# A gMLP and dilated-attention trunk: q stored with bare sums of squares, its statistics made in the attention; layer A's low halves one step later; operand tiles in another order

## The chip, the cores and the metric

The kernel runs on one core of a Trainium2 chip. The metric is the device time of one execution in microseconds (us), as the median over runs. PE is TensorE's matmul side and PEld its weight load, DVE is VectorE, ACT is ScalarE, POOL is GpSimd, and SP is the engine whose queue issues nearly all DMAs of this kernel.

## The reference

One batch of 2048 tokens with 1024 features passes through a gMLP layer A and a layer B of attention in three dilated groups. All is float32. Cut to what matters here:

```python
def gmlp_layer(x, ...):                     # layer A, width 2048
    shift, scale, gate = ada_mod(c, ada_w, ada_b, 3)
    h = rms_norm(x, norm_g) * (1 + scale) + shift
    u, v, z = jnp.split(h @ w_in, 3, axis=-1)
    v = rms_norm(jax.nn.gelu(v), sgu_g)     # then mixed within chunks of 128 tokens
    y = jax.nn.gelu(u) * mixed * jax.nn.silu(z)
    return x + gate * (y @ w_out)

def dilated_layer(x, c, kv_groups, ...):    # layer B; groups (128, 1), (512, 4), (2048, 16)
    shift, scale, gate = ada_mod(c, ada_w, ada_b, 3)
    h = rms_norm(x, norm_g) * (1 + scale) + shift
    qz = h @ w_in                           # 24 heads of 128 for q, then z of 1024
    q = rms_norm(q, q_norm_g) * (HEAD_DIM ** -0.5)
    for g, (window, d) in enumerate(DILATED_GROUPS):
        o, lse = dilated_group_attn(q[:, :, hs], kb, vb, slopes[hs], window, d)
    alpha = softmax(lse over the groups)
    y = sum(alpha * o) * jax.nn.silu(z)
    return x + gate * (y @ w_out)
```

Between them stands one projection to keys and values that all groups of layer B share. The scores of a head are q.k plus minus slope times distance, under a mask of 128 keys. `rms_norm` of q divides each head's row by the root of the mean of its squares plus 1e-6: this is the statistic that the change moves.

## The kernel before

**Blocks and stages.** The 2048 tokens are taken in four blocks of 512, Q = 0 to 3. For each block `layer_A` makes v, u, z, the mixing and the output product; then `proj_B` makes, in this order, `kv_block(2)`, `kv_block(1)`, `q_block(2)`, `kv_block(0)`, `q_block(1)`, `q_block(0)` and `z_block`. A number behind `q_block` is the group of the attention. The q and z projections and layer A's output product are `dense_s`: a product of 2 x 2 blocks with seven products in place of eight, in the order "11", "s2", "12", "s3", "s1", "22", "s4"; its seven operands lie in four large tiles of the pool `big` (`new_ops`), two in a tile. Each product is three matmuls (`mm3`), since operand and weight are each split into a high half and a low half. Layer A's operand is made ahead by `make_hA`, in pieces: `norm_T` transposes and scales two of the eight feature tiles, ACT writes the high half hAh (L615) and DVE subtracts for the low half hAl (L617).

**Weights.** `raw_unit` loads 128 x 512 of a weight into a tile named raw (L264; six buffers), and `split` has ACT copy it to the high half (L255) and DVE subtract for the low half (L259) into a tile named w (eight buffers); the names tell which weight: w_z0b is the z projection of Q = 0, w_q31t of Q = 3 the q projection of group 1. A "t" at such a name's end marks a sum of weight blocks, read from the array wt; in pd_z0bb, the products' sums in PSUM, the last letter tells one of two pairs.

**Storing q.** When `dense_s` has a 128 x 512 piece of q (four heads) it calls `ev` in `q_block`. ACT squares the piece (L1039), DVE sums the squares of each head (L1041), and POOL makes four small operations (L1042 to L1045): times 1/128 plus 1e-6, to the power -0.5, the product of both, and that times the slope. The last results lie in columns 512 to 519 beside the piece, in one tile st of 520 columns. The tile's store to the array qd in HBM goes to a list, `pending`; `flush` (L251) issues what is in the list behind the weight loads of the next product, so on SP the stores of q stand among the loads of weights. SP issues in order: a DMA whose semaphores aren't there yet holds up all behind it. z goes the same way, without statistics.

**The attention.** One unit is a block of 128 queries, four heads. `att_q` loads its qt of 520 columns from qd (L1129), `att_1` transposes it on PE (pq, L1150) and copies the statistics to a small tile rt on DVE (L1160). `att_2` makes the scores (L1182), adds the distance times rt (L1191), takes the maximum (L1194, L1195) and the exponential on ACT (L1201), scaled by rt. `att_3` transposes the result (pp, L1242), and `att_4` multiplies by the values (po, L1261). Groups 0 and 1 of block Q - 1 (`attend_local`) run beside layer A of block Q; group 2, 32 units, runs beside `kv_block(0)`, `q_block(1)` and `q_block(0)` of Q = 3, and block 3's own groups 0 and 1 at the end, in `finish`, with the output projection, whose weights `load_wo` brings from the array wob.

**Who sets the order.** Such work beside the main one is a generator in the list `fillers`; `tick`, called between the matmuls of a dense product, runs so many steps of it as `rate` says. `weave(main, side)` gives a step of the side work to each step of the main one. So the order on every engine follows from where a generator is put in the list, and a scheduler orders what may go beside each other by priority and by the buffers that are free. The gate of layer B, gb, is such side work: `ada_gate` loads eight tiles aw_gb of 128 x 2 x 512 (L170) and sums them on DVE (L172, L174); in this kernel it goes with `proj_B` of Q = 1. `gate_out`, which needs it, is woven into `attend_local(1)`, beside layer A of Q = 2.

Of the kernel before, what the change touches and what calls it, by code (L numbers as in the profile page):

```python
# [12 lines left out]
F32 = mybir.dt.float32  # L13
F32R = mybir.dt.float32r
AF = mybir.ActivationFunctionType
ALU = mybir.AluOpType
AX = mybir.AxisListType

P = 128
# [7 lines left out]
KT = D // P  # L27
# [7 lines left out]
def trunk(ctx, tc, out, x, c, a_ada_w, a_ada_b, a_norm_g, a_w_in, a_sgu_g, a_w_spatial,  # L35
# [204 lines left out]

    wcnt = [0]
    share = [4]
    last_ld = [None]
# [9 lines left out]
    def split(hi, lo, src, pool=False):  # L253

        nc.scalar.activation(hi, src, AF.Copy)  # L255
        i = wcnt[0]
        wcnt[0] += 1
        e = nc.gpsimd if pool or i % share[0] == 3 else nc.vector
        e.tensor_tensor(lo, src, hi.bitcast(F32), ALU.subtract)  # L259
# [333 lines left out]

    def norm_T(xts, pr, outs, nm, ks=range(0, KT, 2), act=False):

        tok = slice(pr * 256, pr * 256 + 256)
        pts = {}
        for oi, (hh, hl, a, b) in enumerate(outs):
            for k2 in ks:
# [7 lines left out]
                for kk in range(2):  # L607
# [4 lines left out]
                    else:  # L612
                        nc.vector.tensor_scalar(h[:, kk, :], pts[k2][:, kk, :], a[:, k:k + 1],
                                                b[:, k:k + 1], ALU.mult, ALU.add)
                nc.scalar.activation(hh[:, k2:k2 + 2, tok], h, AF.Copy)  # L615
                e = nc.gpsimd if act else nc.vector
                e.tensor_tensor(hl[:, k2:k2 + 2, tok], h,  # L617
                                hh[:, k2:k2 + 2, tok].bitcast(F32), ALU.subtract)
        return last

    def new_ops(nm):

        t = [big.tile([P, 2, 2, 4, 256], F32R, tag="big", name=f"ho{nm}{i}") for i in range(4)]
        return {n: (t[i // 2][:, i % 2, 0], t[i // 2][:, i % 2, 1])
                for i, n in enumerate(("11", "12", "22", "s1", "s2", "s3", "s4"))}

# [79 lines left out]
    def make_hA(res, Q, aff):  # L706
# [16 lines left out]
        for t in range(TPQ):  # L723
            nc.vector.tensor_scalar(xts[t], xts[t], r[:, t:t + 1], None, ALU.mult)
            yield
        for pr in range(2):
            for k2 in range(0, KT, 2):
                norm_T(xts[2 * pr:2 * pr + 2], pr, [hA + aff], f"a{Q}_{pr}_", (k2,))
                yield

    def v_evac(Q, m, sqv, j):
# [257 lines left out]
    def proj_B(Q, hk, hb, keep, tail, ahead):  # L989
        def rows(t):  # L990
            return slice((Q * TPQ + t) * P, (Q * TPQ + t + 1) * P)
# [39 lines left out]
        def q_block(g):  # L1031
            def ev(t, src, n):
                if t < 2 and n == 0:
                    c_ = sum_tile(f"qc{g}{Q}{t}")
                    nc.scalar.activation(c_[:, 0:512], src, AF.Copy)
                    src = c_
                nm = f"q{g}{n}{Q}_{t}"
                sq = evt(f"hs_{nm}")
                nc.scalar.activation(sq, src[:, 0:512], AF.Square)  # L1039
                s4 = sp.tile([P, 16], F32, tag="sq", name=f"s4_{nm}")  # L1040
                nc.vector.tensor_reduce(s4[:, 0:4], sq.rearrange("p (h d) -> p h d", d=P), AX.X, ALU.add)  # L1041
                nc.gpsimd.tensor_scalar(s4[:, 4:8], s4[:, 0:4], 1.0 / P, EPS, ALU.mult, ALU.add)  # L1042
                nc.gpsimd.tensor_tensor(src[:, 516:520], s4[:, 4:8], mhalf[:, 0:4], ALU.pow)
                nc.gpsimd.tensor_tensor(s4[:, 4:8], s4[:, 4:8], src[:, 516:520], ALU.mult)
                nc.gpsimd.tensor_tensor(src[:, 512:516], s4[:, 4:8],  # L1045
                                        slopes[:, g * 8 + n * 4:g * 8 + n * 4 + 4], ALU.mult)
                pending.append((qd[g][rows(t), n, :], src))
            dense_s(hb, in_blocks(g), f"q{Q}{g}", ev)
# [8 lines left out]
        ops = make_ops(hb, keep, f"b{Q}")  # L1057
        if Q == 1:
            fillers.append(ada_gate(b_ada_w[0], b_ada_b, 1, "gb"))
        rate[0] = 1.7  # L1060
# [66 lines left out]
    def att_q(g, b, kh):  # L1127
        qt = ap_.tile([P, 520], F32, tag="qt", name=f"qt{g}_{b}_{kh}")
        nc.sync.dma_start(qt, blk_rows(qd[g], g, b)[:, kh, :])  # L1129
        return qt  # L1130

    def att_1(u):

        g, b, kh = u["id"]
        _, nk, _ = geom(g, b)
        if kh == 0:
            pk = pst(f"pk{g}_{b}").rearrange("p (h b j) -> p h b j", h=2, b=2)
# [20 lines left out]
        u["qT"] = qT  # L1158
        rt = sp.tile([P, 16], F32, tag="rt", name=f"rt{g}_{b}_{kh}")
        nc.vector.tensor_copy(rt[:, 0:8], u["qt"][:, 512:520])  # L1160
        u["rt"] = rt

# [153 lines left out]
    def finish():  # L1316
        wo = {}

        def load_wo(n):
            wo[n] = [big.tile([P, KT, 512], F32R, tag="big", name=f"wo{n}{i}") for i in range(2)]  # L1320
            for k in range(0, KT, 2):
                for i in range(2):
                    nc.sync.dma_start(wo[n][i][:, k:k + 2, :].bitcast(F32),
                                      wob[n][i, k * P:(k + 2) * P, :].rearrange("(k p) n -> p k n", p=P))

# [78 lines left out]

        load_wo(0)
        yield
# [6 lines left out]

        yield {"hooks": {4: lambda: load_wo(1)}, "mid": opening}
        drain()
# [49 lines left out]
    fillers.append(side_work())  # L1465
    rate[0], share[0] = 2.2, 1 << 20
    for Q in range(NQ):
        if Q > 0:
            main = attend_local(Q - 1, True)
            fillers.append(weave(main, gate_out()) if Q == 2 else main)  # L1470
            rate[0] = 1.7
# [40 lines left out]
```

## Time and profile before

| what | value |
|---|---|
| runs, us | 3010.62, 3009.8, 3007.87 |
| median, us | 3009.8 |
| profiled execution, its own time, us | 3017.57 |
| its span, us | 3015.4 |
| granted TensorE clock, mean | 0.992 |
| PE busy | 2933.6 us, 97% of the span |
| DVE busy | 2177.0 us, 72% |
| ACT busy | 1682.0 us, 56% |
| POOL busy | 305.5 us, 10% |
| moved by DMA | 609.67 MB, mean 202 GB/s |

The time of an execution is a little longer than the span, which begins and ends with the recorded instructions. Busy shares are means over the whole span; the wait that counts in one stage is seen only there. In the profile's rows a name with an arrow reads "written from read", and L with a number is a line of the kernel. A row of the waits reads: the engine, what it wrote and its line, what it waited for, then the idle us, the number of such waits and the longest. A row of a stretch gives its bounds and length, each engine's busy time with its instructions in brackets, then the granted clock of PE (PEclk, 1.00 is full), the busy share of the DMA engines and GB/s.

### The profile page before, as it was taken

What the parts mean: (1) busy time and instruction counts of PE and PEld (TensorE: products, weight loads), DVE (VectorE), ACT (ScalarE), POOL (GpSimd) and SP (SyncE); (2) the same over time, 40 slices, a digit from 0 to 9 for tenths busy, and PEclk for the clock granted to TensorE, in tenths of its full rate; (3) what the DMA queues carried; (4) which work ended last, traced back from release to release, by engine and by line L of the source; (5) the groups of instructions that cost most, each with busy time, mean ns of one, the idle gap of its engine ahead of it and who ended that gap; (6) DMA issues with size and microseconds to landing.
All of it is one profiled execution on the core that took longest, in us unless ns stands there. A gap on an engine that the chain in (4) does not pass through costs nothing. (4 is left out here: it accounts for less than half of the span.)

```text
span 3015.4 us, 44951 instructions
## 1 busy us (share of the span) xinstructions
PE 2933.6 (97%) x14784; PEld 2465.6 (82%) x14784; DVE 2177.0 (72%) x4180; ACT 1682.0 (56%) x3416; POOL 305.5 (10%) x588
## 2 busy tenths in 40 slices
PE   6999999999999999999999999999999999999999
PEld 4788888778888878778888888788888888887887
DVE  6887576663568787777787876767687876777882
ACT  4333345657456655567465665566466567766540
POOL 4100002320000013400000013200000021120000
PEclk9999999999999999999999999999999999999999
DMA  7899787664433587665633576753333667678752
GB/s 238 272 315 347 247 290 232 221 220 126 141 100 115 170 272 238 211 220 184 222 119 110 189 235 207 247 168 120 120 109 122 210 221 247 223 244 305 244 180 84
DMA packets 372925, 609.67 MB, mean 202 GB/s; under 512 B 38890, under 2 KB 138444, under 8 KB 372692
## 3 DMA queue, kind: packets, MB, share of 16 engines
q1 hardware_dynamic: 372692, 606.80, 61.6%
q8 instruction: 117, 1.92, 0.3%
q14 instruction: 116, 0.95, 0.1%
HBM read 480.18 MB, written 126.49 MB: 201 GB/s over the span
## 5 line engine op out<-in xcount | busy, mean ns | idle before, releaser
L303 PE MATMUL pd_v<-w_v,hAh 128*128 128x512 f32 x1024 | 328.4, 402 | 1.2 <-ACT hAh L615 1.2
L303 PE MATMUL pd_kv<-w_kv,hkh 128*128 128x512 f32 x768 | 239.9, 393 | 0.4
L303 PEld LDWEIGHTS pd_v<-w_v,hAh 128*128 128x128 f32 x1024 | 188.2, 191 | 38.5 <-issue 1.7
L1201 ACT ACTIVATE pr<-pr,stat,rt 128x256 f32<-128x256 f32 (+1 forms) x320 | 177.4, 556 | 54.0 <-DVE stat L1195 33.7
L341 PE MATMUL pd_u<-hAh,w_u 128*128 128x512 f32 x512 | 206.7, 404 | 0.0
L341 PE MATMUL pd_z<-hAh,w_z 128*128 128x512 f32 x512 | 204.4, 399 | 0.0
L303 PE MATMUL pd_v<-w_v,hAl 128*128 128x512 f32 x512 | 202.7, 396 | 0.0
L343 PE MATMUL pd_u<-hAh,w_u 128*128 128x512 f32 x512 | 200.7, 392 | 1.5 <-DVE w_u L259 1.5
L342 PE MATMUL pd_u<-hAl,w_u 128*128 128x512 f32 x512 | 200.1, 391 | 0.0
L343 PE MATMUL pd_z<-hAh,w_z 128*128 128x512 f32 x512 | 200.1, 391 | 0.0
L342 PE MATMUL pd_z<-hAl,w_z 128*128 128x512 f32 x512 | 199.5, 390 | 0.0
L255 ACT ACTIVATE w_u<-raw_u 128x512 fp32r<-128x512 f32 x128 | 79.0, 628 | 172.7 <-PE pd_u L343 94.7
L303 PEld LDWEIGHTS pd_kv<-w_kv,hkh 128*128 128x128 f32 x768 | 143.9, 189 | 31.4 <-DVE w_kv L259 0.9
L255 ACT ACTIVATE w_z<-raw_z 128x512 fp32r<-128x512 f32 x128 | 78.6, 626 | 138.3 <-PE pd_z L343 69.1
L1261 PEld LDWEIGHTS po<-kv,pT 128*128 128x128 f32 x1200 | 147.1, 192 | 9.3 <-ACT pT L1112 2.8
L1261 PE MATMUL po<-kv,pT 128*128 128x128 f32 x1200 | 150.2, 276 | 1.3 <-ACT pT L1112 1.3
L303 PE MATMUL pd_kv<-w_kv,hkl 128*128 128x512 f32 x384 | 150.2, 392 | 0.4 <-DVE hkl L644 0.4
L1191 DVE SCALAR_TENSOR_TENSOR pr<-dist,rt,ps 128x256 f32<-128x256 f32 (+1 forms) x320 | 124.6, 432 | 23.9 <-PE ps L1182 11.9
L259 DVE TENSOR_TENSOR w_u<-raw_u,w_u 128x512 fp32r<-128x512 f32 x128 | 87.1, 687 | 61.6 <-ACT w_u L255 61.4
L255 ACT ACTIVATE w_q<-raw_q 128x512 fp32r<-128x512 f32 x144 | 88.6, 627 | 75.4 <-DMA raw_q<-in_b_w_in_dram 46.8
L237 POOL TENSOR_SCALAR r_b<-sq 128x1 f32<-128x1 f32 x16 | 6.1, 383 | 1196.0 <-DVE sq L889 1195.9
L259 DVE TENSOR_TENSOR w_q<-raw_q,w_q 128x512 fp32r<-128x512 f32 x144 | 95.7, 687 | 41.4 <-ACT w_q L255 40.6
(758 smaller groups left out, 7716.5 us busy)
## 6 DMA issues: line engine op xcount, KB each, us to landing
raw_q<-in_b_w_in_dram SPq DMA_DIRECT2D x144, 256.0 KB
raw_v<-in_a_w_in_dram SPq DMA_DIRECT2D x128, 256.0 KB
raw_u<-in_a_w_in_dram SPq DMA_DIRECT2D x128, 256.0 KB
raw_z<-in_a_w_in_dram SPq DMA_DIRECT2D x128, 256.0 KB
raw_o<-in_a_w_out_dram SPq DMA_DIRECT2D x104, 256.0 KB
qt<-qd SPq DMA_DIRECT2D x96, 260.0 KB
od<-ot SPq DMA_DIRECT2D x96, 256.0 KB
raw_kv<-in_w_kv_dram SPq DMA_DIRECT2D x76, 256.0 KB
```

The costliest lines, as they stand in the source:

```text
L237: nc.gpsimd.tensor_scalar(t[:, 0:n], ssq, 1.0 / width, EPS, ALU.mult, ALU.add)
L255: nc.scalar.activation(hi, src, AF.Copy)
L259: e.tensor_tensor(lo, src, hi.bitcast(F32), ALU.subtract)
L303: last_mm[0] = nc.tensor.matmul(pt, a, u[:, w, :], start=f, stop=e, skip_group_check=more)
L341: nc.tensor.matmul(pts[i], wh, hh[:, k, :], start=k == 0, stop=False)
L342: nc.tensor.matmul(pts[i], wh, hl[:, k, :], start=False, stop=False)
L343: nc.tensor.matmul(pts[i], wl, hh[:, k, :], start=False, stop=k == KT - 1)
L1191: nc.vector.scalar_tensor_tensor(pr[:, i, :], dist[:, 256 - w:256], u["rt"][:, h:h + 1], psc[:, i, :], ALU.mult, ALU.add)
L1201: nc.scalar.activation(pr[:, i, :], pr[:, i, :], AF.Exp, bias=mneg[:, i:i + 1], scale=u["rt"][:, h:h + 1], accum_out=lsum[:, i:i + 1])
L1261: nc.tensor.matmul(po[:, h * P:(h + 1) * P], u["pT"][h // hp][:, h % hp, j, :], u["kv"][:, j, kh, 1, :], start=j == 0, stop=j == nk - 1)
```

## The change

1. q is stored with the bare sums of squares. DVE's sum goes straight to columns 512 to 515 of the tile, the four POOL operations of `q_block` are gone, and the store has 516 columns. `att_1` makes the statistics from the loaded qt, by four POOL operations at its start, and DVE's copy to rt is gone.
2. `norm_T` can put the low half's subtraction in a list; `make_hA` runs each one step after its high half.
3. `new_ops` lays the operands out as "11", "12", "s2", "s3", "22", "s1", "s4".
4. `load_wo` takes one tile of the pool at a time, and the second pair's loads hang at products 2 and 4 of the last z projection, where both hung at 4.
5. The gate gb goes from `proj_B` of Q = 1 to layer A of Q = 1, woven into `attend_local(0)`.
6. `split` no longer counts its calls; POOL makes the low half only where its flag says so.

```diff
 def split(hi, lo, src, pool=False):
         nc.scalar.activation(hi, src, AF.Copy)
-        i = wcnt[0]
-        wcnt[0] += 1
-        e = nc.gpsimd if pool or i % share[0] == 3 else nc.vector
+        e = nc.gpsimd if pool else nc.vector
         e.tensor_tensor(lo, src, hi.bitcast(F32), ALU.subtract)
...
 # norm_T(..., lows=None)
+                def low(k2=k2, h=h):
+                    e = nc.gpsimd if act else nc.vector
+                    e.tensor_tensor(hl[:, k2:k2 + 2, tok], h,
+                                    hh[:, k2:k2 + 2, tok].bitcast(F32), ALU.subtract)
+                if lows is None:
+                    low()
+                else:
+                    lows.append(low)
...
-                for i, n in enumerate(("11", "12", "22", "s1", "s2", "s3", "s4"))}
+                for i, n in enumerate(("11", "12", "s2", "s3", "22", "s1", "s4"))}
...
 # make_hA
+        lows = []
         for pr in range(2):
             for k2 in range(0, KT, 2):
-                norm_T(xts[2 * pr:2 * pr + 2], pr, [hA + aff], f"a{Q}_{pr}_", (k2,))
+                norm_T(xts[2 * pr:2 * pr + 2], pr, [hA + aff], f"a{Q}_{pr}_", (k2,), lows=lows)
+                if len(lows) > 1:
+                    lows.pop(0)()
                 yield
+        lows.pop(0)()
...
 # q_block, ev
-                s4 = sp.tile([P, 16], F32, tag="sq", name=f"s4_{nm}")
-                nc.vector.tensor_reduce(s4[:, 0:4], sq.rearrange("p (h d) -> p h d", d=P), AX.X, ALU.add)
-                nc.gpsimd.tensor_scalar(s4[:, 4:8], s4[:, 0:4], 1.0 / P, EPS, ALU.mult, ALU.add)
-                nc.gpsimd.tensor_tensor(src[:, 516:520], s4[:, 4:8], mhalf[:, 0:4], ALU.pow)
-                nc.gpsimd.tensor_tensor(s4[:, 4:8], s4[:, 4:8], src[:, 516:520], ALU.mult)
-                nc.gpsimd.tensor_tensor(src[:, 512:516], s4[:, 4:8],
-                                        slopes[:, g * 8 + n * 4:g * 8 + n * 4 + 4], ALU.mult)
-                pending.append((qd[g][rows(t), n, :], src))
+                nc.vector.tensor_reduce(src[:, 512:516], sq.rearrange("p (h d) -> p h d", d=P),
+                                        AX.X, ALU.add)
+                pending.append((qd[g][rows(t), n, 0:516], src[:, 0:516]))
...
-        if Q == 1:
-            fillers.append(ada_gate(b_ada_w[0], b_ada_b, 1, "gb"))
...
 # att_q
-        nc.sync.dma_start(qt, blk_rows(qd[g], g, b)[:, kh, :])
+        nc.sync.dma_start(qt[:, 0:516], blk_rows(qd[g], g, b)[:, kh, 0:516])
...
 # att_1
+        rt = u["rt"] = sp.tile([P, 16], F32, tag="rt", name=f"rt{g}_{b}_{kh}")
+        nc.gpsimd.tensor_scalar(rt[:, 12:16], u["qt"][:, 512:516], 1.0 / P, EPS, ALU.mult, ALU.add)
+        nc.gpsimd.tensor_tensor(rt[:, 4:8], rt[:, 12:16], mhalf[:, 0:4], ALU.pow)
+        nc.gpsimd.tensor_tensor(rt[:, 12:16], rt[:, 12:16], rt[:, 4:8], ALU.mult)
+        nc.gpsimd.tensor_tensor(rt[:, 0:4], rt[:, 12:16], slopes[:, g * 8 + kh * 4:g * 8 + kh * 4 + 4],
+                                ALU.mult)
...
-        rt = sp.tile([P, 16], F32, tag="rt", name=f"rt{g}_{b}_{kh}")
-        nc.vector.tensor_copy(rt[:, 0:8], u["qt"][:, 512:520])
-        u["rt"] = rt
...
 # finish
-        def load_wo(n):
-            wo[n] = [big.tile([P, KT, 512], F32R, tag="big", name=f"wo{n}{i}") for i in range(2)]
+        def load_wo(n, i):
+            t = big.tile([P, KT, 512], F32R, tag="big", name=f"wo{n}{i}")
+            wo.setdefault(n, []).append(t)
             for k in range(0, KT, 2):
-                for i in range(2):
-                    nc.sync.dma_start(wo[n][i][:, k:k + 2, :].bitcast(F32),
-                                      wob[n][i, k * P:(k + 2) * P, :].rearrange("(k p) n -> p k n", p=P))
+                nc.sync.dma_start(t[:, k:k + 2, :].bitcast(F32),
+                                  wob[n][i, k * P:(k + 2) * P, :].rearrange("(k p) n -> p k n", p=P))
...
-        yield {"hooks": {4: lambda: load_wo(1)}, "mid": opening}
+        yield {"hooks": {2: lambda: load_wo(1, 0), 4: lambda: load_wo(1, 1)}, "mid": opening}
...
-            fillers.append(weave(main, gate_out()) if Q == 2 else main)
+            fillers.append(weave(main, ada_gate(b_ada_w[0], b_ada_b, 1, "gb") if Q == 1 else
+                                 gate_out()) if Q < 3 else main)
```

The order on SP at the start of the z projection of Q = 0, before, with what each DMA waits for: Pool, DVE and Activation are the engines' semaphores, DMAHW with a number the lanes of the queue itself. st_q00w and st_q00u are pieces of q of group 0, raw_z0b and raw_z0bt weights of the z projection.

```order
L264 DMA raw_z0b_1_5737<-in_b_w_in_dram 128x512 [waits DMAHW2_49,DVE_49]
L251 DMA qd_92<-st_q00w_5461 128x520 [waits DMAHW3_49,Pool_49]
L251 DMA qd_92<-st_q00w_5462 128x520 [waits DMAHW4_49,Pool_49]
L264 DMA raw_z0b_2_5742<-in_b_w_in_dram 128x512 [waits DMAHW5_49,DVE_49,Activation_49]
L251 DMA qd_92<-st_q00u_5231 128x520 [waits DMAHW6_49,DVE_49,Pool_49]
L251 DMA qd_92<-st_q00u_5232 128x520 [waits DMAHW7_49,DVE_49,Pool_49]
L264 DMA raw_z0b_3_5747<-in_b_w_in_dram 128x512 [waits DMAHW0_49,DVE_49,Activation_49]
L264 DMA raw_z0bt_0_5790<-wt_2_117 128x512 [waits DMAHW1_49,DVE_49,Activation_49]
```

The same place on SP after:

```order
L249 DMA qd_92<-st_q00w_5361 128x516 [waits DMAHW2_49,DVE_49]
L249 DMA qd_92<-st_q00w_5362 128x516 [waits DMAHW3_49,DVE_49]
L260 DMA raw_z0b_1_5616<-in_b_w_in_dram 128x512 [waits DMAHW4_49,DVE_49,Activation_49]
L260 DMA raw_z0b_2_5621<-in_b_w_in_dram 128x512 [waits DMAHW5_49,DVE_49]
L249 DMA qd_92<-st_q00u_5151 128x516 [waits DMAHW6_49,DVE_49]
L249 DMA qd_92<-st_q00u_5152 128x516 [waits DMAHW7_49,DVE_49]
L260 DMA raw_z0b_3_5626<-in_b_w_in_dram 128x512 [waits DMAHW0_49,DVE_49,Activation_49]
L260 DMA raw_z0bt_0_5669<-wt_2_117 128x512 [waits DMAHW1_49,DVE_49,Activation_49]
```

The stores keep their place among the loads but for one row, and no longer wait for POOL.

The order on DVE in the attention of group 2, before, at the unit of block 8 (rt_8_1 and qt_8_1 belong to it, rt_7_1 to the unit before):

```order
L1195 SCALAR_TENSOR_TENSOR stat_186<-rt_7_0_24448 128x4
L1110 COPY ot_6_0_24553<-po_6_0_24548 128x512
L259 TENSOR_TENSOR w_q31t_1_24828<-raw_q31t_1_24829,w_q31t_1_24828 128x512
L1160 COPY rt_8_1_24678<-qt_8_1_24584 128x8
L1191 SCALAR_TENSOR_TENSOR b_s<-dist,rt_7_1_24546,ps_7_10_24569 128x128 x4
L1110 COPY kT_8_24589<-pk_8_24586 128x2x128
L1194 TENSOR_REDUCE rt_7_1_24546<-b_s 128x4
```

and on DVE after:

```order
L1197 SCALAR_TENSOR_TENSOR stat_186<-rt_7_0_24222 128x4
L1109 COPY ot_6_0_24335<-po_6_0_24330 128x512
L255 TENSOR_TENSOR w_q31t_1_24612<-raw_q31t_1_24613,w_q31t_1_24612 128x512
L1193 SCALAR_TENSOR_TENSOR b_s<-dist,rt_7_1_24318,ps_7_10_24351 128x128 x4
L1109 COPY kT_8_24376<-pk_8_24373 128x2x128
L1196 TENSOR_REDUCE rt_7_1_24318<-b_s 128x4
```

The copy out of qt_8_1 ahead of the scores of unit 7_1 is gone. On POOL stands after, for the same units, one chain of four behind another:

```order
L1139 TENSOR_TENSOR rt_7_1_24318<-rt_7_1_24318,slopes 128x4
L1136 TENSOR_SCALAR rt_8_0_24368<-qt_8_0_24316 128x4
L1137 TENSOR_TENSOR rt_8_0_24368<-rt_8_0_24368,mhalf 128x4
L1138 TENSOR_TENSOR rt_8_0_24368<-rt_8_0_24368 128x4
L1139 TENSOR_TENSOR rt_8_0_24368<-rt_8_0_24368,slopes 128x4
L1136 TENSOR_SCALAR rt_8_1_24456<-qt_8_1_24366 128x4
```

The first of each chain reads qt, so POOL waits for the load where DVE did.

The order on SP in layer A of Q = 1 after, where the gate's loads (aw_gb) now stand among the v weights (raw_v_0) and the attention's loads of qt:

```order
L1128 DMA qt_1_0_6035<-qd_93 128x516
L170 DMA aw_gb_6049<-in_b_ada_w_dram 128x2x512
L170 DMA aw_gb_6078<-in_b_ada_w_dram 128x2x512
L260 DMA raw_v_0_5_6232<-in_a_w_in_dram 128x512
L1128 DMA qt_1_1_6141<-qd_93 128x516
L170 DMA aw_gb_6125<-in_b_ada_w_dram 128x2x512
L170 DMA aw_gb_6160<-in_b_ada_w_dram 128x2x512
```

Before, they stood in the kv projection of Q = 1, between its weights:

```order
L170 DMA aw_gb_9841<-in_b_ada_w_dram 128x2x512
L170 DMA aw_gb_9875<-in_b_ada_w_dram 128x2x512
L264 DMA raw_kv_0_2_10046<-in_w_kv_dram 128x512
L264 DMA raw_kv_0_3_10052<-in_w_kv_dram 128x512
L888 DMA x1d<-xr_1_8991 128x1024
L264 DMA raw_kv_0_4_10057<-in_w_kv_dram 128x512
L170 DMA aw_gb_9891<-in_b_ada_w_dram 128x2x512
```

In the last z projection the eight loads of wo's second pair stand on SP ahead of the last z weight raw_z3b after:

```order
L1325 DMA wo_25873<-wob_124 128x2x512 x4
L249 DMA zd<-zb_0_25878 128x512
L249 DMA zd<-zb_1_25880 128x512
L1325 DMA wo_25993<-wob_124 128x2x512 x4
L249 DMA zd<-zb_2_26000 128x512
L249 DMA zd<-zb_3_26002 128x512
L260 DMA raw_z3b_0_26059<-in_b_w_in_dram 128x512
```

Before, one of the eight stood ahead of the first two stores of z (zd) and seven behind them, all ahead of the same weight.

More of the change, by code (lines that the diff above doesn't have):

```diff
@@ L239, in rstd_of @@
         return t
-    wcnt = [0]
-    share = [4]
     last_ld = [None]
@@ L592, in ssq_of, with norm_T @@
         return sq[:, 0:1]
-    def norm_T(xts, pr, outs, nm, ks=range(0, KT, 2), act=False):
+    def norm_T(xts, pr, outs, nm, ks=range(0, KT, 2), act=False, lows=None):
         tok = slice(pr * 256, pr * 256 + 256)
@@ L615, in norm_T @@
                 nc.scalar.activation(hh[:, k2:k2 + 2, tok], h, AF.Copy)
-                e = nc.gpsimd if act else nc.vector
-                e.tensor_tensor(hl[:, k2:k2 + 2, tok], h,
-                                hh[:, k2:k2 + 2, tok].bitcast(F32), ALU.subtract)
+                def low(k2=k2, h=h):
[6 more added lines that the diff above has]
+                    lows.append(low)
         return last
@@ L1403, in make_yb @@
                 nc.vector.tensor_tensor(yb[:, 1, ks, :], py, yb[:, 0, ks, :].bitcast(F32), ALU.subtract)
-        load_wo(0)
+        load_wo(0, 0)
+        load_wo(0, 1)
         yield
@@ L1465, in trunk @@
     fillers.append(side_work())
-    rate[0], share[0] = 2.2, 1 << 20
+    rate[0] = 2.2
     for Q in range(NQ):
```

## The prediction

> **What bounds the kernel now.** I read the page's first part, the busy time by stretch, the waits of TensorE (PE), SyncE (SP) and VectorE (DVE), and then the instructions in order of time around the largest gaps. The forecast is made against the profiled execution's own time, 3017.57 us, and carried over as a difference to the median of 3009.8; its span, 3015.4, has 2.2 us around it. A difference within 0.2% (6 us) is no change here: the three runs shown span 2.8 us.
>
> PE is the bound, and all its work is needed:
>
> ```profile
> PE 2933.6 (97%) x14784; PEld 2465.6 (82%) x14784; DVE 2177.0 (72%) x4180; ACT 1682.0 (56%) x3416; POOL 305.5 (10%) x588
> ```
>
> The change takes no matmul out, so only time in which PE stands, or runs at a lower granted clock, can be won. Here are the stretches with such time after the start-up; the columns are length, busy time of PE, PEld, DVE, ACT and POOL, PEclk, DMA share, GB/s:
>
> ```profile
> 580.00:595.00 15.00, 11.75 (x51) 9.12 (x50) 11.16 (x20) 10.54 (x19) 1.23 (x5) 1.00 0.91 309
> 617.00:645.00 28.00, 22.89 (x85) 17.18 (x84) 18.15 (x33) 13.76 (x25) 8.34 (x11) 0.82 0.64 212
> 1222.00:1246.00 24.00, 21.11 (x91) 16.55 (x90) 19.57 (x34) 13.05 (x23) 7.74 (x18) 1.00 0.73 245
> 1282.00:1295.00 13.00, 9.18 (x36) 7.11 (x35) 9.47 (x17) 7.42 (x14) 0.00 (x0) 0.87 0.96 332
> 1900.00:1905.00 5.00, 3.67 (x17) 2.73 (x16) 4.20 (x8) 4.19 (x8) 0.00 (x0) 1.00 1.00 356
> 1930.00:1943.00 13.00, 9.38 (x33) 7.19 (x32) 7.29 (x13) 4.91 (x9) 3.89 (x8) 0.74 0.62 209
> 2494.00:2502.00 8.00, 5.19 (x26) 4.42 (x25) 4.26 (x11) 1.98 (x4) 2.40 (x4) 0.79 0.37 109
> 2576.00:2584.00 8.00, 5.58 (x26) 4.59 (x25) 6.01 (x18) 2.90 (x11) 0.00 (x0) 0.79 0.65 227
> 2619.00:2623.00 4.00, 2.18 (x19) 1.98 (x19) 2.43 (x8) 1.23 (x2) 0.00 (x0) 1.00 1.03 385
> 2637.00:2646.00 9.00, 6.39 (x35) 5.31 (x34) 5.62 (x18) 4.88 (x14) 0.00 (x0) 0.81 0.65 220
> 2726.00:2738.00 12.00, 7.65 (x28) 5.90 (x27) 4.73 (x8) 3.89 (x8) 0.00 (x0) 0.72 1.05 405
> ```
>
> A stretch loses its length less PE's busy time times PEclk: 3.3, 9.2, 2.9, 5.0, 1.3 and 6.1 us in the first six, the ends of the q and z projections of token blocks Q = 0, 1 and 2, together 27.8; then 3.9, 3.6, 1.8 and 3.8 in the attention of group 2 (Q = 3), together 13.1; and 6.5 in the last z projection. Of the first ten's 40.9 us, 11.2 are clock: busy time times one less PEclk.
>
> Why PE stands at 631 and 638 us is seen by following the row that it waited for:
>
> ```profile
> 620.86 0.19 POOL L1042 TENSOR_SCALAR s_q<-s_q 128x4 f32<-128x4 f32 x1 [2.67 <-DVE s_q L1041]
> 621.14 0.67 DVE L1041 TENSOR_REDUCE s_q<-hs_q 128x4 f32<-128x512 f32 x1
> 622.22 4.32 POOL L1044 TENSOR_TENSOR s_q<-s_q,st_q00u 128x4 f32<-128x4 f32 x1
> 626.61 0.20 POOL L1045 TENSOR_TENSOR st_q00u<-s_q,slopes 128x4 f32<-128x4 f32 x1
> 626.84 2.24 SPq L251 DMA_DIRECT2D qd<-st_q00u  x2
> 626.90 0.19 POOL L1042 TENSOR_SCALAR s_q<-s_q 128x4 f32<-128x4 f32 x1
> 627.17 1.01 POOL L1043 TENSOR_TENSOR st_q00u<-s_q,mhalf 128x4 f32<-128x4 f32 x1
> 628.53 0.20 POOL L1045 TENSOR_TENSOR st_q00u<-s_q,slopes 128x4 f32<-128x4 f32 x1
> 629.18 0.37 SPq L264 DMA_DIRECT2D raw_z0b<-in_b_w_in_dram  x1
> 633.14 0.63 ACT L255 ACTIVATE w_z0b<-raw_z0b 128x512 fp32r<-128x512 f32 x1 [8.72 <-DMA raw_z0b<-in_b_w_in_dram]
> 633.82 0.49 PE L303 MATMUL pd_z0bb<-w_z0b,hob 128*128 128x512 f32 x1 [2.19 <-ACT w_z0b L255]
> 620.00:630.00 10.00, 8.81 (x42) 7.04 (x42) 6.48 (x12) 3.80 (x7) 7.31 (x8) 1.00 0.22 76
> ```
>
> Both sums of squares were ready at 621.81, but the stores of q waited for four small POOL operations each and were issued at 626.84 and 628.76. A weight load stood behind them on SP, was issued at 629.18, and its split reached PE late. Meanwhile the DMA engines stood at a share of 0.22. All 96 stores of q wait like this:
>
> ```profile
> SPq L251 <- POOL s_q L1042: 98.6, 34, 8.0
> SPq L251 <- POOL st_qc L1045: 26.9, 14, 3.6
> ```
>
> The gaps of group 2's attention have another releaser: DVE copied the statistics out of each loaded qt, and stood until qt had landed, with the scores of the unit before queued behind.
>
> ```profile
> PE pq L1150 <- DMA qt<-qd: 2.8, 1, 2.8
> ...
> DVE rt L1160 <- DMA qt<-qd: 40.6, 19, 6.4
> ...
> L1160 DVE COPY rt<-qt x96: 158/172/180, 586.3 to 2881.2; 128x8 f32<-128x8 f32 x96
> 2577.99 0.17 DVE L1160 COPY rt<-qt 128x8 f32<-128x8 f32 x1 [5.42 <-DMA qt<-qd]
> 2578.07 1.12 DVE L1191 SCALAR_TENSOR_TENSOR b_s<-dist,rt,ps 128x128 f32<-128x128 f32 x4
> 2579.24 0.66 PE L1242 MATMUL pp<-ident,pr 128*128 128x128 f32 x4 [2.42 <-DVE b_s L1191]
> ```
>
> **The change part by part.** (1) Stores of q. The four POOL operations go out of the store's way; it now waits for the reduce alone. At 626.84 that is 5.0 us earlier (both reduces done at 621.81), at 628.76 6.9 us, and the loads behind move up alike, into the stretch with the idle DMA. What is late next is the DMA itself: in the stretches with a share of 0.91 and more (580, 1282 and 1900 us; 3.3 + 5.0 + 1.3 = 9.6 us) the same bytes must still pass. I take half of those 9.6 and all of the other 18.2: 23 us. Ends: 0 and 27.8. The store of 516 instead of 520 columns is under 1% of its bytes: nothing.
>
> (2) The attention. 96 copies of 0.172 us leave DVE (16.5 us, all beside PE's work: nothing by itself), and with them the head-of-line waits of 40.6 us in this stage. POOL now waits for qt and makes the statistics. The three stretches at 2576, 2619 and 2637 us (9.2) follow this pattern. At 2494 PE itself waits 2.8 us for the first qt (the row of pq), whose load follows the last stores of q; these come earlier by (1), so I take half, 2. What the same units will wait for next I bound by that row's 2494 stretch, 3 us: 9.2 + 2 - 3 = 8. Ends: 0 and 13.1. The new POOL chain is 1.83 us when undisturbed (626.90 to 628.73), against the time that the first scores left after the copy:
>
> ```profile
> 2497.74 0.17 DVE L1160 COPY rt<-qt 128x8 f32<-128x8 f32 x1 [6.36 <-DMA qt<-qd]
> 2502.32 1.12 DVE L1191 SCALAR_TENSOR_TENSOR b_s<-dist,rt,ps 128x128 f32<-128x128 f32 x4 [0.25 <-PE ps L1182]
> ```
>
> 4.6 us, so it costs nothing while POOL is undisturbed. In layer A the loaded qt lies ready for longer.
>
> The 4.32 us of L1044 against 0.20 is POOL standing while DVE (busy 6.48 of those 10 us) ran one two-input subtraction after another. The Trainium skill (SBUF — State Buffer, Who interferes with whom) says that a DVE instruction with two SBUF inputs shuts out a GpSimd one that reads SBUF for its whole length. By that rule an operation waits for one DVE instruction; here it waited for a whole run of them, and the measured 4.32 us decides.
>
> (3) The gate's weights (gb). Eight DMAs of 512 KB and their DVE work leave Q = 1's kv projection for the start of layer A of Q = 1, between the attention's steps and ahead of its kv loads on SP:
>
> ```profile
> L174 DVE SCALAR_TENSOR_TENSOR acc_gb<-aw_gb,sc,acc_gb x14: 731/746/753, 1083.4 to 1110.5; 128x512 f32<-128x512 f32 x14
> L172 DVE TENSOR_SCALAR acc_gb<-aw_gb,sc x2: 480/483/486, 1082.9 to 1097.5; 128x512 f32<-128x512 f32 x2
> 1050.00:1100.00 50.00, 48.10 (x219) 37.43 (x218) 43.78 (x78) 28.74 (x61) 4.46 (x8) 1.00 0.78 255
> 1710.00:1760.00 50.00, 48.79 (x229) 39.86 (x228) 38.16 (x68) 27.27 (x56) 3.79 (x8) 1.00 0.76 258
> 650.00:700.00 50.00, 50.00 (x252) 41.92 (x251) 27.06 (x56) 34.98 (x69) 0.00 (x0) 1.00 0.55 179
> ```
>
> Where they were, PE lost 1.9 us, and 1.2 in the same place of Q = 2 without them: 0.7 won. Where they go, 14 x 0.746 + 2 x 0.483 = 11.4 us of DVE work meet 22.9 idle us, and 4.2 MB meet a DMA share of 0.55. DVE now waits there for these landings with weight splits behind it. Ends: a win of 1.9, and a loss of 17, eight waits of 2.1 (40.6 / 19, as for qt). I take a loss of 2, a stretch like 2619's, since DVE and DMA have room.
>
> (4) Layer A's low halves one step later: the waits of this row go at best, so 0 to 3.2; I take 0, since weight loads and not these end the gaps.
>
> ```profile
> DVE hAl L617 <- ACT hAh L615: 3.2, 2, 1.8
> ```
>
> (5) Operand tiles in another order, wo loaded tile by tile: the gap at 2728 us had the last z weights behind eight wo loads on SP, at a DMA share of 1.05, and the order of after still has all eight ahead of them. 0, at best 6.5. (6) The share counter in `split` took POOL only where the flag does already: 0.
>
> Sum: 23 + 8 - 2 = 29 us; 3017.6 becomes 2988.6, and the median 3009.8 becomes 2981.
>
> The clock term is weighed too. The Trainium skill (TensorE: Matmul & The Clock Gate, What's actually happening) has the half clock follow an idle window of about 3.4 us; here one gap of 2.42 us already left a PEclk of 0.79 at 2576. By that rule such gaps would cost no clock, and the 40.9 us to be won would be near 33; the measured clock decides.
>
> **The rivals.** *The DMA decides.* If the ends of the projections are bound by bytes, earlier issues only move the gap: for it the shares of 0.91 to 1.05, against it 0.22 just before. A quarter of 27.8 is left: 7 + 8 - 2 = 13, 2997 us.
>
> *The gate stalls layer A.* The loss end of (3): 29 + 2 - 17 = 14, 2996 us. For it, DVE's waits for qt; against it the 22.9 idle us.
>
> *All of it, and the wo gap too*: 27.8 + 13.1 + 1.9 = 43, and some of 6.5 in place of what is missed: 2967 us.
>
> *No earlier loads.* If SP's next load waits for a raw buffer anyway, the store's wait was none: nothing from (1), and (2) less (3) makes 6, of which half is lost again: 3007 us. Against it the weight load 0.34 us behind the last store.
>
> *Slower: POOL becomes the attention's bound.* If DVE's runs stretch every chain as at 622 us (620.86 to 626.81, 6.0 us from the first reduce), the scores come 6.0 - 4.6 = 1.4 us late in each of group 2's 32 units, 45 us, which turns 29 won into 16 lost: 3026 us. It decides from 0.9 us a unit, a chain of 5.5. For it: DVE is busy 6.0 of 8 us there. Against it: the very next chain took 1.83 us beside the same DVE work. By the Trainium skill's rule of the shut-out (SBUF — State Buffer, Who interferes with whom), with the gate's 0.75 us for one two-input instruction, a chain would take 1.83 + 4 x 0.75 = 4.8 us: an estimate, 0.2 late a unit and 7 us in all, short of the point from which this rival decides.
>
> **How the numbers follow.** The forecast gets 0.52, the DMA rival 0.16, the gate 0.10, all of it 0.10, no earlier loads 0.06, slower 0.06. The first four are faster by over 0.2%: 0.88; no earlier loads is the 0.06 within it. The range reaches from everything at its best (27.8 + 13.1 + 1.9 + 3.2 = 46: 2964) to the DMA rival with part of the gate's loss, 2964 to 3004.
>
> **What would show it.** Right: the waits of SP's q stores for POOL gone; the stretches 617, 1282 and 1930 with PEclk near 1 and DMA near even; no wait of DVE for qt. (2) fails if scores wait for POOL's rt; (3) if PE or DVE waits for aw_gb after 650 us. Wrong overall: the same gaps at the same weights though the stores come earlier, or new gaps behind POOL.

## The result, and the profile after

The changed kernel takes 2959.76 us (median of 4 runs, 2959.06 to 2963.5) against 3009.34 us before (4 runs, 3007.87 to 3010.62): a ratio of 0.9838, 95% interval [0.9825, 0.9851], or 45 to 53 us won. The prediction said 2981, with 2964 to 3004 as its range. The direction and the first mechanism were right; the size was not, and the time lies 4 us below the range.

The first part of the page after, the same row that was shown of before:

```profile
PE 2910.5 (98%) x14784; PEld 2454.7 (83%) x14784; DVE 2169.8 (73%) x4084; ACT 1686.6 (57%) x3416; POOL 290.6 (10%) x588
```

PE has the same 14784 matmuls, in 23 us less of busy time. A PE at half clock counts as busy: at 626.91 us of before, at a granted clock of 1.00, six matmuls of a product took 1.52 us, and at 638.55, at 0.50, six took 2.90. The mean granted clock went from 0.992 to 0.998.

Here are the places that answer to the stretches at 580, 617, 1282, 1900 and 2726 us of before, each at the same distance from the first matmul of its projection (columns as there):

```profile
580.70:595.70 15.00, 15.00 (x68) 12.40 (x67) 11.94 (x19) 10.07 (x18) 2.05 (x4) 1.00 0.86 283
613.70:641.70 28.00, 28.00 (x134) 23.16 (x133) 24.80 (x43) 17.84 (x31) 0.00 (x0) 1.00 0.81 258
1262.60:1275.60 13.00, 13.00 (x63) 10.72 (x62) 10.79 (x19) 7.57 (x13) 0.00 (x0) 1.00 0.79 269
1873.50:1878.50 5.00, 5.00 (x23) 4.14 (x23) 3.83 (x6) 4.11 (x8) 0.00 (x0) 1.00 0.73 218
2675.70:2687.70 12.00, 12.00 (x63) 9.97 (x62) 9.45 (x14) 8.15 (x21) 1.60 (x4) 1.00 1.01 381
```

PE is busy in all of each stretch, at full clock. The DMA share is lower than before in the three that the forecast took for bound by bytes (0.86, 0.79 and 0.73 against 0.91, 0.96 and 1.00). Over the last one it is 1.01, and PE loses nothing.

The instructions in order of time at the start of the z projection of Q = 0, the place that was followed at 621 to 634 us of before:

```profile
611.47 0.69 DVE L1046 TENSOR_REDUCE st_q00u<-hs_q 128x4 f32<-128x512 f32 x1
...
612.19 1.37 SPq L249 DMA_DIRECT2D qd<-st_q00u  x2
612.53 0.67 DVE L1046 TENSOR_REDUCE st_q00u<-hs_q 128x4 f32<-128x512 f32 x1
...
614.32 0.33 SPq L260 DMA_DIRECT2D raw_z0b<-in_b_w_in_dram  x1
```

The first store goes out 0.03 us after its reduce, both are issued by 613.56, and the weight load behind them is issued 1.1 us after the second reduce, where it took 7.4 before (621.81 to 629.18).

To see where the time came from, the program is cut into stages at the first matmul of each projection, in each trace. "Projections" is q_block(1), q_block(0) and z_block of Q = 0, 1 and 2; "attention" is kv_block(0), q_block(1) and q_block(0) of Q = 3, beside which group 2 runs; "last z" goes from the first matmul of the last z projection to the start of the last matmul of all. Lengths in us, of the kernels before and after and of some of the experiments below:

| stage | before | E2 | E4 | E6 | E1 | E5 | E7 | after |
|---|---|---|---|---|---|---|---|---|
| projections | 386.9 | 383.7 | 385.4 | 381.4 | 354.4 | 354.4 | 354.4 | 354.4 |
| attention | 207.8 | 200.3 | 201.9 | 193.5 | 192.8 | 192.5 | 191.8 | 191.7 |
| last z | 321.1 | 321.0 | 319.4 | 320.2 | 313.0 | 310.4 | 311.9 | 313.3 |

The profiled execution of before (3017.57 us) was a long one: on the chip of E1 to E4, 27 runs of that kernel lie between 3001.67 and 3015.85. Its traces' difference, 58 us, therefore overstates the medians' 50. With the mean of the four traces whose projections are as before (386.9, 383.7, 385.4, 381.4: 384.4) the projections give 30.0 us. The attention gives 11.1: 203.3, the mean of before, E2, E4 and of E3's 203.3, less 192.2, the mean of E1, E5, E7 and after. The last z gives 8.5: 320.6, the mean of before, E2, E6 and of E3's 320.1, less 312.1. That is 49.6, as much as the medians differ by (49.58). So close a match is luck: the attention alone varies by 7.5 us among the four traces that have no part of q's change, and the last z by 2.9 among the four that do.

### The profile page after: what moved, and what is told of

It reads as the page before. It is cut to its first block, busy times and chain, and to the rows that moved or that the text cites. A ratio compares the mean times of both kernels' runs of the same rounds, so it can differ in the third digit from the quotient of the medians.

```text
span 2957.4 us, 44909 instructions
## 1 busy us (share of the span) xinstructions
PE 2910.5 (98%) x14784; PEld 2454.7 (83%) x14784; DVE 2169.8 (73%) x4084; ACT 1686.6 (57%) x3416; POOL 290.6 (10%) x588
## 5 line engine op out<-in xcount | busy, mean ns | idle before, releaser
L299 PEld LDWEIGHTS pd_v<-w_v,hAh 128*128 128x128 f32 x1024 | 188.5, 191 | 40.6 <-issue 3.5
L339 PE MATMUL pd_u<-hAh,w_u 128*128 128x512 f32 x512 | 200.3, 391 | 2.0 <-DVE w_u L255 2.0
L1136 POOL TENSOR_SCALAR rt<-qt 128x4 f32<-128x4 f32 x96 | 27.7, 289 | 1189.2 <-DMA qt<-qd 992.0
L253 ACT ACTIVATE w_o<-raw_o 128x512 fp32r<-128x512 f32 x104 | 64.3, 628 | 101.2 <-PE pd_o L299 39.9
L255 DVE TENSOR_TENSOR w_v<-raw_v,w_v 128x512 fp32r<-128x512 f32 x120 | 81.1, 695 | 50.5 <-ACT w_v L253 50.4
```

The source lines that it names most:

```text
L299: last_mm[0] = nc.tensor.matmul(pt, a, u[:, w, :], start=f, stop=e, skip_group_check=more)
L339: nc.tensor.matmul(pts[i], wl, hh[:, k, :], start=False, stop=k == KT - 1)
```

## The experiments

**Which part carries it: E1 to E4, one part each on the kernel before.** E1 is the statistics of q alone:

```diff
 # q_block, ev: reduce into src[:, 512:516], store 516 columns, no POOL
 # att_1: the four POOL operations from qt, no copy on DVE; all else as before
```

> The statistics of q alone: bare sums stored, POOL's chain in the attention, DVE's copy gone; the rest as before. Theory A (the queue and the copy carry nearly all): the q and z projections of the first three blocks lose the 32 us that the traces of before and after differ by there, and group 2's attention the 16 us; the time falls by 40 to 48 us, to about 2965. Rival B (the forecast's sizes were right and the rest comes from the small parts): it falls by 31 us, 23 and 8, to about 2978.

Measured: 2963.91 us, ratio 0.9851 [0.9838, 0.9865]. Theory A fits. The projections fall to the 354.4 us that the changed kernel has, and the last z falls as well, with wo still loaded in the old way:

```profile
2645.38:2690.38 45.00, 44.97 (x211) 37.14 (x210) 30.50 (x47) 26.17 (x48) 1.61 (x4) 1.00 1.00 358
```

That is the first 45 us of E1's last z projection: a DMA share of 1.00, and PE busy for 44.97 us. The same 45 us before:

```profile
2690.18:2735.18 45.00, 39.79 (x174) 31.80 (x173) 30.00 (x48) 24.82 (x47) 8.02 (x16) 0.94 0.96 334
```

E2 moves the gate alone.

```diff
-            fillers.append(weave(main, gate_out()) if Q == 2 else main)
+            fillers.append(weave(main, ada_gate(b_ada_w[0], b_ada_b, 1, "gb") if Q == 1 else
+                                 gate_out()) if Q < 3 else main)
```

> Only the gate gb is moved to layer A of Q = 1. Theory A: the kv projection of Q = 1 becomes 3.5 us shorter and the v stage of Q = 1 2 us longer, a win of 1 to 2 us. Rival (the forecast): a loss of 2 us. A rival C in which POOL's chains in the way made room for it: alone, with q's stores still waiting for POOL, a loss of 3 or more.

Measured: 3007.69 us, 0.9994 [0.9985, 1.0003]: no change. In E2's trace, as in that of the whole change, the kv projection of Q = 1 is 3.5 us shorter (46.65 and 46.67 us, where before had 50.17) and the v stage 2.3 longer. Here are the 109.41 us of that v stage in the whole change, and the 107.10 before:

```profile
651.04:760.45 109.41, 109.41 (x561) 90.67 (x560) 54.37 (x109) 76.18 (x162) 17.40 (x36) 1.00 0.50 159
```

```profile
664.65:771.75 107.10, 107.10 (x557) 90.41 (x556) 44.02 (x99) 76.48 (x162) 1.76 (x4) 1.00 0.40 126
```

PE is busy throughout in both. The 2.3 us are the gate's own four matmuls of 0.59 us, which moved with it, and no wait. What was won is the other 1.2 us, in which PE stood in the kv projection; that is too little to show in the time. In the v stage DVE waited for the gate's weights, and PE did not stand for it:

```profile
DVE acc_gb L174 <- DMA aw_gb<-in_b_ada_w_dram: 2.4, 3, 1.0
```

E3 runs layer A's low halves one step later, and nothing else.

```diff
 # make_hA, cut: each low half is kept in lows and made one step later
+                if len(lows) > 1:
+                    lows.pop(0)()
```

> Only layer A's low halves one step later. Theory A and the forecast: 0, since the waits for hAl were 3.2 us in all and beside others; at best 3 us. Rival B: 5 us or more, since the low halves run on DVE ahead of weight splits at the ends of the projections, where make_hA runs, and a DVE instruction that waits for ACT holds up the splits.

Measured: 3001.55 us, 0.9980 [0.9970, 0.9990]: 3 to 9 us faster, 5.8 by the median, which is rival B's size and more than the forecast's 0 to 3.2. In its trace the projections take 379.5 us, 4.9 less than the mean of 384.4 above; z_block of Q = 1 takes 42.85 us (before, E2, E4, E6: 46.9, 45.6, 47.5, 45.2). So the win lies in the projections; that it comes about as rival B says, by splits that DVE no longer holds up, was not followed in the trace. E11 below shows what becomes of it.

E4 lays the operand tiles in the other order and loads wo tile by tile.

```diff
 # new_ops and load_wo as in the change; of finish:
-        yield {"hooks": {4: lambda: load_wo(1)}, "mid": opening}
+        yield {"hooks": {2: lambda: load_wo(1, 0), 4: lambda: load_wo(1, 1)}, "mid": opening}
```

> Only the order of the operand tiles and wo loaded tile by tile. Theory A: the gap of 4.6 us (with its half clock 6.8) ahead of the last z product goes, since the last z weights are issued 4 to 6 us earlier: 5 to 7 us won, all in the last z projection. The forecast: 0, since all eight loads of wo still stand ahead of those weights.

Measured: 3008.92 us, 0.9999 [0.9990, 1.0008]: no change, and theory A fell. The first 45 us of its last z projection have the same gaps as before, and SP's queue waits for POOL there as before:

```profile
2680.59:2725.59 45.00, 40.23 (x175) 32.12 (x174) 30.60 (x48) 25.06 (x47) 7.62 (x16) 0.96 0.95 331
```

```profile
SPq L251 <- POOL s_q L1042: 4.3, 3, 3.0
...
SPq L251 <- POOL st_q30w L1045: 2.0, 1, 2.0
...
SPq L251 <- POOL st_q30v L1045: 1.5, 1, 1.5
SPq L251 <- POOL st_q30u L1045: 1.5, 1, 1.5
```

These are the stores of q_block(0) of Q = 3, which stand at the start of the last z projection: 9.3 us in which SP issued no weight. E1 takes these waits away and the gap goes; E4 leaves them and it stays. The loads of wo that stood next to the late weights were not its cause.

**Wait or work: E5, E6 and E7.** E5 frees the stores but leaves DVE's copy out of each qt, now with POOL's chain behind it.

```diff
 # q_block and att_q as in E1; at the end of att_1:
+        nc.vector.tensor_copy(rt[:, 12:16], u["qt"][:, 512:516])
+        nc.gpsimd.tensor_scalar(rt[:, 12:16], rt[:, 12:16], 1.0 / P, EPS, ALU.mult, ALU.add)
 # then the other three on POOL, as in att_1 after
```

> Half of q's part: the bare sums are stored, so the stores wait for DVE alone, but DVE still copies the sums out of each qt ahead of the scores, and POOL's chain follows the copy. Theory A (two independent queues): the projections' ends and the last z projection keep their whole win as with q's part alone (32 and 8 us), the attention of group 2 none of its 15; some 33 us faster than before by the median. Rival D (the waits for qt came from the late stores): the attention wins as well, 43 us as with all of q's part. Rival E: the chain behind the copy makes the attention slower by 1 us a unit, so under 10 us are left.

Measured: 2960.95 us, 0.9842 [0.9829, 0.9856]. Rival D fits, not A: the attention wins its 11 us too (192.5). Its waits for qt, in the stages of group 2, are these:

```profile
DVE rt L1155 <- DMA qt<-qd: 21.6, 16, 4.6
```

DVE still waits, half as long as the 40.6 us before, and PE hardly stands: it is busy for 190.45 of 193.00 us there.

E6 is the other half: the stores wait as before, and POOL makes the copy.

```diff
-        nc.vector.tensor_copy(rt[:, 0:8], u["qt"][:, 512:520])
+        nc.gpsimd.tensor_copy(rt[:, 0:8], u["qt"][:, 512:520])
```

> The other half: the kernel before, with the copy of the statistics out of qt made by POOL instead of DVE. Stores wait as before. Theory A: no projection changes; DVE's waits for qt are gone, 8 to 15 us won in the attention of group 2. Rival D: nothing, since the scores wait for the same landing by way of POOL.

Measured: 2999.11 us, 0.9965 [0.9952, 0.9977]: 7 to 14 us faster, nearly all of it in the attention (193.5), as A had it. Now it is POOL that waits for the late qt:

```profile
POOL rt L1160 <- DMA qt<-qd: 72.9, 20, 7.3
```

So two things together made the attention's gaps: loads of qt that came late on a queue held up by stores, and DVE, which stood at its head for each of them. Either taken away is enough (192.5 us in E5, 193.5 in E6), and taken away together they give no more (192.8 in E1).

E7 is E1 with the POOL operations still made in the projections, into a tile that nobody reads.

```diff
                 pending.append((qd[g][rows(t), n, 0:516], src[:, 0:516]))
+                s4 = sp.tile([P, 16], F32, tag="sq", name=f"s4_{nm}")
+                nc.gpsimd.tensor_scalar(s4[:, 4:8], src[:, 512:516], 1.0 / P, EPS, ALU.mult, ALU.add)
 # ... and the other three, into s4
```

> q's part alone, and besides the four POOL operations of each piece stay in the projections, writing to a tile that nobody reads: the work is there, the wait of the store is not. Theory A (it is the wait): as with q's part alone, 2964 us, within 2 us. Rival F (POOL's work itself slows DVE's splits beside it): most of the 32 us come back, 2990 or more.

Measured: 2960.38 us, 0.9838 [0.9824, 0.9851]. It is the wait, in the last z as well (311.9). Its q_block(0) and z_block of Q = 0:

```profile
569.03:608.08 39.05, 39.05 (x177) 32.32 (x176) 36.16 (x60) 26.73 (x46) 24.39 (x45) 1.00 0.87 290
608.08:649.08 41.00, 41.00 (x193) 33.89 (x192) 35.73 (x61) 26.32 (x45) 9.94 (x12) 1.00 0.80 256
```

POOL is busy for 24.39 of 39.05 us, more than before in that place (17.58), and PE has no gap.

**How long POOL's chain may be: E8 and E12.** Four, then three more powers of 1.0 us stand in each chain of the attention, on E1's base; their results are not read.

```diff
         nc.gpsimd.tensor_tensor(rt[:, 4:8], rt[:, 12:16], mhalf[:, 0:4], ALU.pow)
+        for _ in range(4):          # 3 in E12
+            nc.gpsimd.tensor_tensor(dead[:, 0:4], rt[:, 12:16], mhalf[:, 0:4], ALU.pow)
```

> q's part alone, with four more powers of 1.0 us, to a tile that nobody reads, inside each chain of the attention: a chain of some 5.9 us undisturbed in place of 1.83. Theory A with the forecast's limit of 4.6 us: 1.3 us late in each of 32 units of group 2, up to 40 us slower than q's part alone. Rival G (POOL works a whole step ahead, since att_1 of a unit comes a step before its scores and qt lies ready): under 5 us slower.

Measured: 3018.06 us, 1.0025 [1.0014, 1.0036], 57.7 us above E7 on the same chip. The attention takes 246.0 us, 54.2 more than E7's, 1.69 for each of 32 units: rival G fell, and A's 40 us was too little. POOL works chain after chain there: from 2460 to 2688 us it pauses once, for 2.5 us, and DVE's scores wait for it:

```profile
2539.08 1.01 POOL L1134 TENSOR_TENSOR rt<-rt,mhalf 128x4 f32<-128x4 f32 x1
2540.06 4.26 POOL L1136 TENSOR_TENSOR dead<-rt,mhalf 128x4 f32<-128x4 f32 x4
2544.39 0.20 POOL L1137 TENSOR_TENSOR rt<-rt 128x4 f32<-128x4 f32 x1
2544.67 0.54 POOL L1138 TENSOR_TENSOR rt<-rt,slopes 128x4 f32<-128x4 f32 x1
2545.30 0.19 POOL L1133 TENSOR_SCALAR rt<-qt 128x4 f32<-128x4 f32 x1
```

```profile
DVE b_s L1192 <- POOL rt L1138: 24.0, 10, 3.0
```

> q's part with three more powers in each chain of the attention, 4.9 us undisturbed. Theory L (a chain may take 4.6 us before the scores are late, as the forecast had it): 0.3 to 0.7 us in each of 32 units, 10 to 22 us slower than q's part alone. Theory T (POOL is a resource with a rate: a chain must only be shorter than a unit, and 32 units take 193 us, 6.0 each; with four powers a chain took 6.2 to 6.5): within 4 us of q's part alone.

Measured: 2985.65 us, 0.9920 [0.9906, 0.9934], 26.0 us above E10 on the same chip. The attention takes 214.0 us, 21.8 above E10's 192.2, 0.68 a unit: the size of theory L at its upper end, which the time itself passes, and T's forecast fell. T's mean of 6.0 us a unit was taken over a stage in which units are not spread evenly:

```profile
2494.00:2586.43 92.43, 91.06 (x633) 82.16 (x632) 74.67 (x181) 79.48 (x229) 34.54 (x77) 1.00 0.86 281
2586.43:2647.88 61.45, 61.45 (x378) 54.11 (x377) 51.10 (x113) 50.74 (x138) 14.07 (x32) 1.00 0.79 251
```

These are q_block(1) and q_block(0) of E10, where POOL does little but these chains of four: 77 instructions are some 19 chains, one in 4.8 us, and 32 are 8, one in 7.7. The two lengths of chain differ by one power, 1.007 us, and by 1.01 us a unit. So past its limit each us of chain costs a us a unit; going back from E12 by 0.68 sets the limit at 1.83 + 3 x 1.007 - 0.68 = 4.2 us of undisturbed chain, an estimate from two points.

POOL's own rows say what sets it. These are one chain of E12 and the first row of the next:

```profile
2535.58 0.19 POOL L1133 TENSOR_SCALAR rt<-qt 128x4 f32<-128x4 f32 x1
2535.86 1.01 POOL L1134 TENSOR_TENSOR rt<-rt,mhalf 128x4 f32<-128x4 f32 x1
2536.83 3.60 POOL L1136 TENSOR_TENSOR dead<-rt,mhalf 128x4 f32<-128x4 f32 x3
2540.51 0.20 POOL L1137 TENSOR_TENSOR rt<-rt 128x4 f32<-128x4 f32 x1
2540.78 0.20 POOL L1138 TENSOR_TENSOR rt<-rt,slopes 128x4 f32<-128x4 f32 x1
2541.07 0.19 POOL L1133 TENSOR_SCALAR rt<-qt 128x4 f32<-128x4 f32 x1
```

The next chain begins 0.09 us behind the last, and so it goes on: from 2456 to 2651 us POOL makes 34 chains of 5.4 us in the mean with one pause of over 0.6 us (3.5 us, at 2515). But for that pause qt lay ready, and POOL did not keep up. In E10 the same 34 chains begin 4.85 us apart in the mean, and POOL pauses ahead of 30 of them. So theory T had the mechanism right, POOL as a resource with a rate, and its limit wrong: a chain has to fit into the 4.85 us at which E10's units come, not into 6.0. That agrees with the 4.2: E12's chains took some 0.55 us more in this stage than undisturbed (5.4 against 1.83 + 3 x 1.007), and 4.2 + 0.55 is 4.75.

**What the rest is worth on top: E9, E10 and E11, on one chip.** E9 is the changed kernel, E10 is E1 once more, E11 is E1 with E3's edit.

> The changed kernel once more, beside q's part alone on the same chip, to see what the other five parts are worth on top of it. Theory A (q's part is nearly all): 0 to 3 us faster than q's part alone. Rival B (the small parts add up: low halves 5.8, gate 1, wo 1): 6 us or more faster.

> q's part alone once more, on the same chip as the changed kernel: 0.984 to 0.986 of the kernel before.

> q's part with the low halves one step later. Theory A (the low halves alone won their 5.8 us in the same gaps that q's part closes): within 2 us of q's part alone, and the stages of the q and z projections, already without a gap there, unchanged. Rival B (a win of their own): 4 to 6 us faster than q's part alone.

Measured: 2963.53, 2959.62 and 2963.03 us; 0.9847 [0.9834, 0.9861], 0.9840 [0.9824, 0.9856] and 0.9848 [0.9834, 0.9861]. The medians lie within 4 us and each kernel's own runs spread over 5 to 10, so the three can't be told apart: the other five parts together are worth nothing that these runs can measure on top of q's. The projections are 354.4 us in each trace. What E3 won was in the stages whose gaps q's part closes, and is not won twice.

## Why the prediction was right or wrong

- **The stores of q, step (1): the right mechanism, 23 us forecast, 30.0 measured.** The step that failed reads "in the stretches with a share of 0.91 and more ... the same bytes must still pass. I take half". A high share just behind a late issue was the queue catching up, not a limit: with the issue on time the same places run at 0.73 to 0.86 with no gap, and those 12 us of the last z at 1.01 with none. The rival "the DMA decides" fell with it. The stretches listed also missed small gaps beside them: this trace lost 386.9 - 354.4 = 32.5 us there, not 27.8.
- **The last z projection, step (5): 0 forecast, 8.5 measured.** This is the second step that failed. The prediction itself said that all 96 stores wait like this (its two rows hold 48 waits; in the trace 92 of the 96 wait for POOL, 206 us in all), and applied it to three blocks of four. In the last block it looked at what stood next to the late weights on SP, the wo loads, and asked whether their order changed. It did not ask since when the queue was late. E1 and E4 settle it. On the tiles and on wo themselves 0 was right.
- **The attention, step (2): 8 forecast, 11.1 measured,** within its ends of 0 and 13.1. Of the 3 us set aside for a next wait most came, since PE still waits 2.2 us in that stage after; the half taken of the 2494 stretch was too little, for PE's wait for the first qt there is gone. Scores wait for POOL's rt, the sign of failure that it named, once in these stages after, for 1.4 us. The story was incomplete: the copy on DVE was blamed, and E5 shows that with the copy left in place the gaps go as well.
- **The gate, step (3): a loss of 2 forecast, a win of 1.2 in the trace, nothing in the time.** The wait of DVE for its loads came as forecast (4.3 us in the v stage, 2.4 of them in the row shown), but DVE is idle for half of that stage, and PE is busy through all of it. The rival built on it fell.
- **Low halves (4): 0 was right for the change as a whole,** and too low for the edit alone, which wins 3 to 9 us while the stores are late.
- **The clock.** To count the half clock behind the gaps as time to be won was right: of the traces' 58 us about 18 are clock, an estimate worked out from the means as 3015.4 x 0.008 less 2957.4 x 0.002. The stretches at half clock behind the gaps of the projections, of group 2's attention and of the last z's start are all gone after.
- **The range.** Its lower end was the sum of all best ends, 46 us, but with the last z at 0 in it. The rival "all of it, and the wo gap too" had 2967 with a chance of 0.10; what happened is that rival with 8.5 us in the last z, though not by way of wo. Set against a profiled execution 8 us above the median, even the carried-over gaps were a little large; the misses above outweighed that.
- **"Slower: POOL becomes the attention's bound" is real, but not at 1.83 us.** The forecast put the limit at 4.6 us, as a date of the scores; the runs put it near 4.2, as POOL's pace. Its argument against this rival was misread: the chain that took 1.83 us at 626.90 did not stand beside the same DVE work, since DVE was idle from 626.48 to 633.80. What bears against it is E10, where chains beside DVE's work in group 2 are as short: 14.07 us for the eight in its last row above.
- **"No earlier loads"** fell: the load behind the stores is issued 6.3 us sooner, and PE has it in time.

The waits after show the rest. POOL's idle time for qt is long and harmless, and the stores of q no longer wait for POOL. Of their long waits, those for DVE's reduce are left, the longest 3.5 us; this is the row with the most of them:

```profile
POOL rt L1136 <- DMA qt<-qd: 992.0, 63, 72.3
```

```profile
SPq L249 <- DVE st_qc L1046: 11.3, 21, 1.0
```

## What to carry to other kernels

A store on an in-order queue should wait for as little as possible: here four small operations on POOL, 1.8 to 6 us, cost PE 38 us through the loads behind the stores that waited for them, and E7 shows that the same work off the store's path costs nothing. When a gap lies behind a high DMA share, ask first whether the queue was late before it; here a share of 0.91 to 1.00 after a stall was the queue catching up. A mechanism found in one stage is priced in every stage that issues the same instructions, and of two parts that cure the same gap only one pays. Work that is moved to an idle engine has to fit the pace at which it is asked for while it runs, not an average over a longer stage.

## What the runs showed that was not expected

One POOL power took 1.007 us as a rule, but up to 2.9 us in E8:

```profile
L1136 POOL TENSOR_TENSOR dead<-rt,mhalf x384: 998/1007/2922, 583.1 to 2889.2; 128x4 f32<-128x4 f32 x192
```

The longest began at 1409.12 us of E8 and took 2.92 us; DVE's rows there are these:

```profile
1408.68 1.28 DVE L260 TENSOR_TENSOR w_u<-raw_u,w_u 128x512 fp32r<-128x512 f32 x2
1409.88 0.69 DVE L423 TENSOR_TENSOR w_go<-rawo,w_go 128x512 fp32r<-128x512 f32 x1
1410.49 0.68 DVE L260 TENSOR_TENSOR w_u<-raw_u,w_u 128x512 fp32r<-128x512 f32 x1
```

The Trainium skill (SBUF — State Buffer, Who interferes with whom) has a GpSimd instruction blocked for the whole of a DVE instruction with two SBUF inputs. The power took 1.9 us more than usual and ended 0.9 us behind a run of four such instructions of some 0.69 us, and the 4.32 us at 622.22 of before ended 0.06 us behind a run of seven: in these traces POOL was kept out for several instructions in a row.
